# A two-layer RG-LRU and attention backbone with grouped experts: one written order past the end of the first experts, another order of the second layer's experts, and quarters of the output tiles for small blocks

## The chip, the cores and the metric

The kernel runs on one core of one Trainium2 chip. The metric is the device time of one execution in microseconds (us), lower is better. The names of the engines: PE multiplies matrices (TensorE), DVE is VectorE, ACT is ScalarE, POOL is GpSimd, SP is SyncE. SP only issues DMAs here; POOL issues the indirect DMAs (gathers and scatters) beside its own arithmetic.

## The reference, cut to what matters

Two layers over 256 latent tokens and 256 context tokens of 1024 numbers each, in float32. Layer 0 mixes with a recurrent block, layer 1 with grouped-query attention (the context is only read there). Behind each mixer stands a mixture of 16 experts, of which a router picks two for every token; the experts of layer 1 see the latent tokens alone.

```python
for i in range(DEPTH):                                     # DEPTH = 2
    hx = modulate(x, norm_mix_w[i], sh_m, sc_m)
    ...
    dx, dc = rglru_mixer(...) if i == 0 else attention_mixer(...)
    x = x + g_m * dx
    ...
    hx = modulate(x, norm_ffn_w[i], sh_f, sc_f)
    ...
    x = x + g_f * grouped_moe(hx, router_w, router_b, moe_w1[i], moe_w3[i], moe_w2[i])

def grouped_moe(h, router_w, router_b, w1, w3, w2):
    ...                                                    # gates: two of 16 experts per token, the others 0
    for e in range(N_EXPERTS):
        y = y + gates[..., e:e + 1] * ((jax.nn.silu(h @ w1[e]) * (h @ w3[e])) @ w2[e])
    return y
```

## The kernel before

**Layers and stages.** The program runs layer 0's mixer (to about 300 us), layer 0's experts (to about 608), layer 1's attention (`enter` and `Heads`, to about 790) and layer 1's experts (to the end). All weights are read once from HBM, in tiles of 2 MB, in two halves each, on SP's queue in one fixed order of jobs. A half is issued when its tile is free and when the fourth half before it has landed (`AHEAD = 4`).

**Experts.** The router's counts are known only at run time, so every expert place `e` has a fixed room. The first places (three in layer 0, four in layer 1) hold the experts 0 to 2 or 0 to 3. The others are filled by rank, the most wanted expert first: `ORDERS` says which rank stands at which place, `ROOM` how many rows a rank has room for, and `AGAIN` which ranks may have 128 rows more, in a branch (`tc.If`) that is skipped when it isn't needed. In layer 1 ranks 0 and 1 have room for 160 rows, worked as a block of 128 rows and a block of 32; every other rank has one block of 32 rows, and the four first places have one of 64. The places from 12 on are only worked if their expert has a token.

**One expert.** `fetch` clears a tile and gathers the expert's rows from HBM (POOL), `turn` transposes them (PE, with copies on ACT and DVE), `ups` multiplies by w1 and w3 (PE, line 945, tile `up`), ACT and DVE form the product `sx`, `flips` transposes it (PE) and copies it back (DVE, line 959), and `downs` multiplies by w2 (PE, line 977, tile `py`). DVE then multiplies with the gate into a tile `y` (line 985 in layer 1, line 988 in layer 0) and POOL adds these rows into HBM with an indirect DMA, the scatter (line 991). In the loop of `run`, place `e` does its `ups`, then the `downs` of place `e - 1`, then its own `flips`; places `e + 2` to `e + 5` are prepared in between.

**Scatters.** A scatter adds into the tensor that the scatter before it adds into, so each waits for the one before it to land. It reads `y`, so DVE may write that part of `y` again only when the scatter has landed. In layer 1 there are two such tiles, `ys[0]` and `ys[1]` (rows 2 and 3 of the tile `xr`, which is the name that the profile gives them), and `row` picks one of them.

**What sets the order.** Inside a `manual_schedule` region an engine runs its instructions in the order of the source; outside, a scheduler orders them by its own estimates. Each engine works its queue strictly in order. Through the experts the order of DVE, ACT, POOL and SP is manual, and PE's too.

**Between the layers.** After the last expert of layer 0, `leftover` holds work for rooms that were too small (skipped here). `enter` then splits the key and value weights (the third part of `qkv`) into a high and a low part, in eight pieces: `parts` copies a piece to `wkv` (ACT, line 1335) and subtracts for `wkvl` (DVE and POOL in turn, line 1336). SP loads the sums of layer 0 back from HBM (line 1364, `y<-yr`) once the last scatter has landed; DVE and POOL multiply them with a gain (line 1371), and the key and value products follow. The split of the query weights (`wq`, `wql`) is on ACT and POOL as well.

Of the kernel before, what the change touches and what calls it, by code (L numbers as in the profile page):

```python
# [15 lines left out]
ET = mybir.EngineType  # L16

D = 1024
NK = 8
# [15 lines left out]
ADA_AT = [32, 34]  # L35


ORDERS = [[11, 0, 10, 1, 9, 2, 8, 3, 7, 4, 6, 5, 12], [0, 2, 1, 3, 4, 5, 6, 7, 8, 9, 10, 11]]
ROOM = [[192, 128, 96, 96, 96, 96, 64, 64, 64, 64, 64, 64, 32], [160, 160, 32] + 9 * [32]]

AGAIN = [[1, 2, 3, 4, 6], [2, 3]]
# [21 lines left out]
BLOCKS = {0: (128, [(0, 0, 0)]), 1: (64, [(1, 0, 1)]), 2: (32, [(2, 0, 2)]), 3: (96, [(1, 0, 1), (2, 64, 3)])}  # L63
# [3 lines left out]
def base(i, k):  # L67

    return BASE if k < FIRST[i] else ROOM[i][ORDERS[i][k - FIRST[i]]]


def again(i, k):

    return k < FIRST[i] or ORDERS[i][k - FIRST[i]] in AGAIN[i]

# [12 lines left out]
def hybrid_kernel(ctx: ExitStack, tc: tile.TileContext, x, c, ctxt, c_ctx, ada_w, ada_b, norm_mix_w, norm_ffn_w,  # L88
# [3 lines left out]
    nc = tc.nc  # L92
# [5 lines left out]
    def open_banks(name):  # L98
        banks["ctx"] = ExitStack()
        banks["pool"] = banks["ctx"].enter_context(tc.tile_pool(reuse_waits="tile", name=name, bufs=8, space=PSUM))  # L100
# [72 lines left out]
    def done(key, more=True):  # L173
        pool = live.pop(key)[1]
        if more and (pool is not state.get("brief") or state["sent"] < LAST):
            send(pool)
        elif not more and state.get("later"):
            owed.append(pool)
# [390 lines left out]
    with tc.tile_pool(reuse_waits="tile", name="big0", bufs=1) as bp:  # L569
# [29 lines left out]
        with tc.tile_pool(reuse_waits="tile", name="n0", bufs=2) as n0, \  # L599
# [9 lines left out]
            parts = wp.tile([128, 4096], F32R, tag="w", name="parts")  # L609
# [101 lines left out]
        with tc.tile_pool(reuse_waits="tile", name="o0", bufs=2) as op:  # L711
            R0 = Router(0, [0, 1, 2, 3], op)
            pinned = tc.manual_schedule(engines={ET.PE})
# [7 lines left out]
    def moe(R, after=None):  # L721
        with ExitStack() as ctx2:
            if after is not None:
                state["brief"] = ctx2.enter_context(tc.tile_pool(reuse_waits="tile", name="weights0", bufs=1))
                send(state["brief"])
            moe_(R, ctx2.enter_context(tc.tile_pool(reuse_waits="tile", name=f"route{R.i}", bufs=1, side="right")),
                 after is not None)
        pinned.__exit__(None, None, None)
        if after is not None:

            for k in (("w1", E - 2), ("w3", E - 2), ("w2", E - 2), ("w1", E - 1)):
                done((k[0], R.i, k[1]), False)
            after(R.yr)

    def moe_(R, rp, early):
        i, chunks, conds, hr, yr, lg = R.i, R.chunks, R.conds, R.hr, R.yr, R.lg
# [4 lines left out]
        def places():  # L741

            xg = [rp.tile([128, D], F32, name=f"xg{a}") if i == 0 or a == 2 else xr[:, a, :] for a in range(NX)]
            xh = rp.tile([128, D], F32, name="xh")
            sx = [rp.tile([128, FF], F32, name=f"sx{a}") if i == 0 or a > 1 else None for a in range(4)]
            ys = [rp.tile([128, D], F32, name=f"y{a}") for a in range(3)] if i == 0 else [xr[:, 2 + a, :] for a in range(2)]
            for t in xg + sx[0:2] if i == 0 else []:
                nc.gpsimd.memset(t, 0.0)
            return xg, xh, sx, ys

        if i == 0:
            xg, xh, sx, ys = places()
# [86 lines left out]
        if i == 1:  # L839
            R.gf = rp.tile([128, D], F32, name="gf")  # L840
            xg, xh, sx, ys = places()
        ps1v = ps1.rearrange("p (c e) -> p c e", c=C)
        work = ExitStack()
# [116 lines left out]

        def row(e, b, bk):

            return ys[(e + b) % 2] if i or b == 0 else ys[2]

        def down(bk, aT, W2, ls, b, e):
# [136 lines left out]
            banks.pop("spare")  # L1102

        other = beside()
        work.enter_context(tc.manual_schedule(engines={ET.DVE, ET.Activation, ET.Pool, ET.SP}))
        warm = wk.tile([128, 1], F32, name="warm", bufs=1)
        busy(2)
        lists(0)
# [185 lines left out]
                    block(k, nk, room(i, k))  # L1294

        leftover()
        work.close()
        open_banks(f"psum{i + 1}")


    actx = ExitStack()

    def spare(name, dt=F32R):
        return wp.tile([128, 4096], dt, tag="w", name=name)

    def enter(yr):
# [13 lines left out]
        def wide(name, dt=F32R):  # L1320
            return spare(name, dt).rearrange("p (k f) -> p k f", k=NK)

        wkv, wkvl, hhi = wide("wkv"), wide("wkvl"), wide("hhi")
# [5 lines left out]
        ys = [misc[:, 1024 * z:1024 * z + 1024] for z in range(2)] + [yp.tile([128, D], F32, name=f"y{z}") for z in (2, 3)]  # L1329
        A, B = scale_vec(1, SC_M, 96, "am1"), vec(1, SH_M)  # L1330

        def parts(key, hi, lo, k, low):

            w = take(key).rearrange("p (k f) -> p k f", k=NK)[:, k, :]
            nc.scalar.activation(hi[:, k, :], w, AF.Copy)
            low.tensor_sub(lo[:, k, :], w, hi[:, k, :])

        with tc.manual_schedule(engines={ET.PE, ET.Activation, ET.DVE, ET.Pool}):
            for k in range(NK):
                parts(("qkv", 2), wkv, wkvl, k, (nc.vector, nc.gpsimd)[k % 2])  # L1340
            for j in (1, 0):
                spread(gf[j], vec(0, G_F), j)

# [303 lines left out]
    with ExitStack() as _:  # L1647
        with tc.tile_pool(reuse_waits="tile", name="o1", bufs=2) as op:
            R1 = Router(1, [2, 3], op)
            pinned = tc.manual_schedule(engines={ET.PE})  # L1650
# [8 lines left out]
def _constants():  # L1659
# [30 lines left out]
    for i in range(2):  # L1690
        k = FIRST[i]
        a[:, C_KEY + 16 * i:C_KEY + 16 * i + 16] = np.where(x < k, 65536 + 16384 * (k - 1 - x), E - 1 - x)
        a[:, C_RANK + 16 * i:C_RANK + 16 * i + 16] = list(range(k)) + [k + r for r in ORDERS[i]]
        a[:, C_ROOM + 16 * i:C_ROOM + 16 * i + 16] = [room(i, k) for k in range(E)]
# [32 lines left out]
```

## Time and profile before

| | |
|---|---|
| median of 3 runs | 1015.61 us (1012.28 to 1016.7) |
| the profiled execution, its own time | 1015.41 us |
| its span, first to last instruction | 1013.7 us |
| mean granted clock of PE, share of full | 0.927 |
| PE busy | 854.2 us, 84% |
| DVE busy | 488.6 us, 48% |
| ACT busy | 299.5 us, 30% |
| POOL busy | 252.4 us, 25% |
| HBM read and written | 290.85 MB and 14.81 MB, 302 GB/s over the span |

All times in the rows are from the span's start. The time beside the span, 1015.41 against 1013.7, is start and end that the trace does not show. An engine with a high busy share may still wait in single stages, so the shares say little about a change that acts in one stage; for that the waits and the timeline of the stage are read.

### The profile page before, as it was taken

The numbers are of one execution on the slowest core, as the hardware profiler recorded it, in microseconds if no ns is written. First come the engines' busy times: TensorE is split into PE (matmuls) and PEld (weight loads), VectorE is DVE, ScalarE is ACT, GpSimd is POOL, SyncE is SP. The second block draws the span as 40 slices with busy tenths as digits, with TensorE's granted clock in tenths as the row PEclk, the third lists the DMA queues.
The fourth block names the chain that finished last, engine by engine and source line by source line (L and its number), as shares of the span: only waits on it lengthen the run. The fifth ranks groups of instructions, "written<-read, shape, count | busy, mean of one in ns | idle before, by whom it ended". The sixth has DMA issues, their size and how long they took to land. (4 is left out here: it accounts for less than half of the span.)

```text
span 1013.7 us, 17132 instructions
## 1 busy us (share of the span) xinstructions
PE 854.2 (84%) x6495; PEld 538.8 (53%) x6495; DVE 488.6 (48%) x1366; ACT 299.5 (30%) x549; POOL 252.4 (25%) x193
## 2 busy tenths in 40 slices
PE   3789899889996999999998743879999689989953
PEld 2357675574454555456554413768654545545632
DVE  2878796652258632132221024587942664243452
ACT  3346556672012110011010012646851311110100
POOL 2272233300003320111211133652430223132232
PEclk9799999999997999999999967899999789999977
DMA  9956964899415899999999944221959589998970
GB/s 346 357 163 214 387 229 166 306 386 376 176 63 203 301 363 383 364 359 355 347 355 375 367 151 150 99 89 59 361 173 398 182 304 378 341 372 274 375 276 10
DMA packets 126926, 277.11 MB, mean 273 GB/s; under 512 B 7673, under 2 KB 12889, under 8 KB 126816
## 3 DMA queue, kind: packets, MB, share of 16 engines
q1 hardware_dynamic: 116064, 253.77, 68.4%
q0 software_dynamic: 8880, 15.54, 6.6%
q10 hardware_dynamic: 1872, 6.37, 1.6%
q8 instruction: 64, 1.05, 0.4%
q14 instruction: 46, 0.38, 0.1%
HBM read 290.85 MB, written 14.81 MB: 302 GB/s over the span
## 5 line engine op out<-in xcount | busy, mean ns | idle before, releaser
L945 PE MATMUL up<-w,xg 128*32 128x128 f32 (+2 forms) x1984 | 161.4, 338 | 10.1 <-DMA w<-in_moe_w_dram 9.4
L977 PE MATMUL py<-w,sx 128*32 128x256 f32 (+2 forms) x768 | 130.1, 521 | 19.1 <-DVE sx L959 17.9
L945 PEld LDWEIGHTS up<-w,xg 128*32 128x32 f32 (+2 forms) x1984 | 104.6, 127 | 60.4 <-issue 24.3
L950 DVE TENSOR_TENSOR sx<-sx,up 128x256 f32<-128x256 f32 (+3 forms) x31 | 13.4, 434 | 176.0 <-PE up L945 94.1
L977 PEld LDWEIGHTS py<-w,sx 128*32 128x32 f32 (+2 forms) x768 | 45.6, 135 | 84.9 <-issue 56.0
L949 ACT ACTIVATE sx<-up 128x256 f32<-128x256 f32 (+3 forms) x31 | 12.2, 395 | 230.5 <-PE up L945 217.5
L585 POOL TENSOR_TENSOR parts<-w,parts 128x1024 fp32r<-128x1024 f32 x16 | 40.3, 2520 | 113.0 <-DVE parts L584 105.0
L945 PE MATMUL up<-w,xr 128*32 128x128 f32 (+2 forms) x640 | 63.4, 351 | 0.6 <-ACT xr L508 0.6
L991 POOL DMA_INDIRECT yr<-y,yi x21 | 32.8, 1563 | 106.3 <-DVE y L988 37.1
L531 PE MATMUL bank<-w,yT 128*128 128x512 f32 x128 | 57.3, 595 | 0.0
L182 PE MATMUL bank<-hhi,parts 128*128 128x512 f32 x128 | 52.8, 412 | 4.2 <-DVE hhi L399 4.2
L183 PE MATMUL bank<-hlo,parts 128*128 128x512 f32 x128 | 52.1, 407 | 4.2 <-DVE hlo L400 2.2
L184 PE MATMUL bank<-hhi,parts 128*128 128x512 f32 x128 | 51.8, 405 | 1.3 <-POOL parts L585 1.3
L945 PEld LDWEIGHTS up<-w,xr 128*32 128x32 f32 (+2 forms) x640 | 38.5, 132 | 22.3 <-issue 15.6
L917 POOL DMA_INDIRECT xg<-hr,gi x21 | 20.8, 989 | 116.1 <-DVE f L908 67.9
L316 PE MATMUL bank<-w,st 128*32 128x512 f32 x384 | 46.4, 615 | 3.6 <-DMA w<-in_ada_w_dram 3.3
L932 ACT ACTIVATE xg<-tp 128x512 f32<-128x512 f32 x32 | 17.4, 594 | 84.8 <-PE tp L927 84.8
L465 DVE TENSOR_TENSOR rt<-bank,gm 128x512 f32<-128x512 f32 x12 | 8.3, 692 | 66.9 <-PE bank L531 66.9
L988 DVE TENSOR_SCALAR y<-py,gt 128x512 f32<-128x512 f32 (+1 forms) x21 | 14.4, 687 | 51.6 <-PE py L977 51.6
L985 DVE SCALAR_TENSOR_TENSOR xr<-py,gt,gf 32x256 f32<-32x256 f32 (+2 forms) x44 | 24.4, 554 | 30.6 <-PE py L977 19.7
L991 POOL DMA_INDIRECT out_dram<-xr,yi x14 | 22.1, 1581 | 64.4 <-DVE xr L985 19.6
L531 PEld LDWEIGHTS bank<-w,yT 128*128 128x128 f32 x128 | 23.4, 190 | 25.7 <-issue 25.5
(360 smaller groups left out, 1630.1 us busy)
## 6 DMA issues: line engine op xcount, KB each, us to landing
w<-in_moe_w_dram SPq DMA_DIRECT2D x192, 1024.0 KB
w<-in_ada_w_dram SPq DMA_DIRECT2D x48, 1024.0 KB
w<-in_lru_in_w_dram SPq DMA_DIRECT2D x8, 1024.0 KB
w<-in_attn_qkv_w_dram SPq DMA_DIRECT2D x6, 1024.0 KB
w<-in_lru_out_w_dram SPq DMA_DIRECT2D x4, 1024.0 KB
w<-in_attn_o_w_dram SPq DMA_DIRECT2D x4, 1024.0 KB
hr<-h ACTq DMA_DIRECT2D x6, 512.0 KB
yr<-zero POOLq DMA_DIRECT2D x4, 512.0 KB, 10.8
```

Source lines behind the costliest of these rows:

```text
L182: nc.tensor.matmul(pb, wh, xh, start=start, stop=False, skip_group_check=True)
L183: nc.tensor.matmul(pb, wh, xl, start=False, stop=False, skip_group_check=True)
L184: nc.tensor.matmul(pb, wl, xh, start=False, stop=stop, skip_group_check=True)
L316: nc.tensor.matmul(pa[32 * g:32 * g + 32, :], st[:, 4 * r + g, :], w[:, 4 * r + g, :], start=r == 0, stop=r == 1, skip_group_check=True, t ...
L531: nc.tensor.matmul(pb, src[:, k, n * 128:(n + 1) * 128], w[:, k, :], start=k == 0, stop=k == NK - 1)
L585: nc.gpsimd.tensor_sub(lo, w, h)
L917: nc.gpsimd.indirect_dma_start(out=dst[0:rows, :], out_offset=None, in_=hr[:, :], in_offset=bass.IndirectOffsetOnAxis(ap=idx[0:rows, :], a ...
L932: nc.scalar.activation(dst, pb, AF.Copy)
L945: nc.tensor.matmul(pw[g * Tn:(g + 1) * Tn, at:at + fg], hT[:, k, t0:t0 + Tn], W[:, k, g * fg:(g + 1) * fg], start=k == 0, stop=k == NK - 1 ...
L977: nc.tensor.matmul(py[j * Tn:(j + 1) * Tn, 0:wd], aT[:, ao + q * 128 + g * Tn:ao + q * 128 + (g + 1) * Tn], W2[:, f, j * dg + h * 512:j * ...
L985: nc.vector.scalar_tensor_tensor(dst[ps, :], py[ps, 0:wd], gate[ps, :], R.gf[ps, at:at + wd], ALU.mult, ALU.mult)
L991: nc.gpsimd.indirect_dma_start(out=yr[:, :].rearrange("r (g f) -> (r g) f", g=G), out_offset=bass.IndirectOffsetOnAxis(ap=ls.yi[:, z, b:b ...
```

## The change

Four edits. The order of DVE, ACT, POOL and SP in layer 0 stays manual beyond the experts, through `leftover` and the split of the key and value weights in `enter`, and so does PE's; the split thereby stands behind the experts' last instruction on each engine. In layer 1 the ranks stand in another order: the two ranks with 160 rows are at places 6 and 8 in place of 4 and 6, and the two with a branch at places 4 and 5 in place of 5 and 7. In layer 1 a block of 32 rows, which is 256 columns wide in `y`, goes into a quarter of `ys[e % 2]` that moves on with `e`, in place of the first 256 columns of `ys[(e + b) % 2]` (`b` is the block's number in its expert).

```diff
--- before.py
+++ after.py
@@ -35,7 +35,7 @@
 ADA_AT = [32, 34]
 
 
-ORDERS = [[11, 0, 10, 1, 9, 2, 8, 3, 7, 4, 6, 5, 12], [0, 2, 1, 3, 4, 5, 6, 7, 8, 9, 10, 11]]
+ORDERS = [[11, 0, 10, 1, 9, 2, 8, 3, 7, 4, 6, 5, 12], [2, 3, 0, 4, 1, 5, 6, 7, 8, 9, 10, 11]]
 ROOM = [[192, 128, 96, 96, 96, 96, 64, 64, 64, 64, 64, 64, 32], [160, 160, 32] + 9 * [32]]
 
 AGAIN = [[1, 2, 3, 4, 6], [2, 3]]
@@ -725,8 +725,9 @@
                 send(state["brief"])
             moe_(R, ctx2.enter_context(tc.tile_pool(reuse_waits="tile", name=f"route{R.i}", bufs=1, side="right")),
                  after is not None)
-        pinned.__exit__(None, None, None)
-        if after is not None:
+        if after is None:
+            pinned.__exit__(None, None, None)
+        else:
 
             for k in (("w1", E - 2), ("w3", E - 2), ("w2", E - 2), ("w1", E - 1)):
                 done((k[0], R.i, k[1]), False)
@@ -960,6 +961,9 @@
 
         def row(e, b, bk):
 
+            if i == 1 and BLOCKS[bk] == BLOCKS[2]:
+
+                return ys[e % 2][:, e // 2 % 4 * 256:]
             return ys[(e + b) % 2] if i or b == 0 else ys[2]
 
         def down(bk, aT, W2, ls, b, e):
@@ -1102,7 +1106,7 @@
             banks.pop("spare")
 
         other = beside()
-        work.enter_context(tc.manual_schedule(engines={ET.DVE, ET.Activation, ET.Pool, ET.SP}))
+        region.enter_context(tc.manual_schedule(engines={ET.DVE, ET.Activation, ET.Pool, ET.SP}))
         warm = wk.tile([128, 1], F32, name="warm", bufs=1)
         busy(2)
         lists(0)
@@ -1294,11 +1298,15 @@
                     block(k, nk, room(i, k))
 
         leftover()
+        if i == 1:
+            region.close()
         work.close()
         open_banks(f"psum{i + 1}")
 
 
     actx = ExitStack()
+
+    region = ExitStack()
 
     def spare(name, dt=F32R):
         return wp.tile([128, 4096], dt, tag="w", name=name)
@@ -1335,9 +1343,11 @@
             nc.scalar.activation(hi[:, k, :], w, AF.Copy)
             low.tensor_sub(lo[:, k, :], w, hi[:, k, :])
 
+        for k in range(NK):
+            parts(("qkv", 2), wkv, wkvl, k, (nc.vector, nc.gpsimd)[k % 2])
+        region.close()
+        pinned.__exit__(None, None, None)
         with tc.manual_schedule(engines={ET.PE, ET.Activation, ET.DVE, ET.Pool}):
-            for k in range(NK):
-                parts(("qkv", 2), wkv, wkvl, k, (nc.vector, nc.gpsimd)[k % 2])
             for j in (1, 0):
                 spread(gf[j], vec(0, G_F), j)
```

Three places in the order of instructions, as the two programs hold them (numbers of lines differ by 1 to 10 between the two, by what the diff adds).

DVE at the end of layer 0's experts, before: `wkvl` is the split, `sx<-pa` with 256 and 128 columns the `flips` of place 14, `y` the products for the scatters of places 14 and 15.

```order
L988 TENSOR_SCALAR y_2083<-py,gt 128x512
L1162 UNCONDITIONAL_BRANCH x2
L1336 TENSOR_TENSOR wkvl<-w,wkv 128x512 x2
L959 COPY sx_2077<-pa 128x256
L959 COPY sx_2077<-pa 128x128
L1336 TENSOR_TENSOR wkvl<-w,wkv 128x512 x2
L950 TENSOR_TENSOR sx_2078<-sx_2078,up 128x128
L988 TENSOR_SCALAR y_2081<-py,gt 128x512
L988 TENSOR_SCALAR y_2081<-py,gt 128x256
L959 COPY sx_2078<-pa 128x128
L988 TENSOR_SCALAR y_2082<-py,gt 128x256
```

The same place on DVE after the change:

```order
L992 TENSOR_SCALAR y_2083<-py,gt 128x512
L1166 UNCONDITIONAL_BRANCH x2
L960 COPY sx_2077<-pa 128x256
L960 COPY sx_2077<-pa 128x128
L951 TENSOR_TENSOR sx_2078<-sx_2078,up 128x128
L992 TENSOR_SCALAR y_2081<-py,gt 128x512
L992 TENSOR_SCALAR y_2081<-py,gt 128x256
L960 COPY sx_2078<-pa 128x128
L992 TENSOR_SCALAR y_2082<-py,gt 128x256
```

The two pairs of `wkvl` instructions are gone from between the experts' instructions; they come behind the branch of `leftover`.

POOL from the end of `leftover` on, before: `misc` is the gain, `hlo` the low part of the modulated tokens (the second `hlo` belongs to the second 128 latent tokens), `wql` the split of the query weights.

```order
L1371 TENSOR_TENSOR misc<-misc 128x1024 x2
L1405 TENSOR_TENSOR hlo_11878<-m,hhi 128x4x128
L1336 TENSOR_TENSOR wql<-w,wq 128x512 x6
L1405 TENSOR_TENSOR hlo_11878<-m,hhi 128x4x128
L1336 TENSOR_TENSOR wql<-w,wq 128x512 x6
L1405 TENSOR_TENSOR hlo_11878<-m,hhi 128x4x128
```

The same place on POOL after the change:

```order
L1344 TENSOR_TENSOR wkvl<-w,wkv 128x512 x4
L1381 TENSOR_TENSOR misc<-misc 128x1024 x2
L1415 TENSOR_TENSOR hlo_11876<-m,hhi 128x4x128
L1344 TENSOR_TENSOR wql<-w,wq 128x512 x8
L1415 TENSOR_TENSOR hlo_11876<-m,hhi 128x4x128
L1344 TENSOR_TENSOR wql<-w,wq 128x512 x3
L1415 TENSOR_TENSOR hlo_11876<-m,hhi 128x4x128
```

The four `wkvl` instructions stand here now, and the second `hlo` stands behind eight `wql` instructions in place of six.

DVE at the second expert with 160 rows in layer 1, with the semaphores that an instruction waits for in brackets (`DMASW` are those of POOL's DMAs), before: place 6, two halves of the block of 128 rows, then four pieces of the block of 32, then the `flips` of place 7.

```order
L985 SCALAR_TENSOR_TENSOR xr<-py,gt,gf 128x512 [waits DMASW6_49,DMASW1_49,PE_49]
L985 SCALAR_TENSOR_TENSOR xr<-py,gt,gf 128x512 [waits PE_49]
L985 SCALAR_TENSOR_TENSOR xr<-py,gt,gf 32x256 [waits DMASW5_49,PE_49]
L985 SCALAR_TENSOR_TENSOR xr<-py,gt,gf 32x256 x3
L959 COPY sx_13475<-pa 128x128 [waits PE_49]
L882 CAST r_15425<-ls 128x5 [waits PE_49]
L867 TENSOR_SCALAR oh<-io_b,psp 128x128 x2
L950 TENSOR_TENSOR sx_13473<-sx_13473,up 128x128 [waits PE_49,Activation_49]
```

The same after the change, at place 8:

```order
L989 SCALAR_TENSOR_TENSOR xr<-py,gt,gf 128x512 [waits PE_49]
L989 SCALAR_TENSOR_TENSOR xr<-py,gt,gf 128x512 [waits DMASW1_49,PE_49]
L989 SCALAR_TENSOR_TENSOR xr<-py,gt,gf 32x256 [waits DMASW5_49,DVE_49,PE_49]
L989 SCALAR_TENSOR_TENSOR xr<-py,gt,gf 32x256 x3
L960 COPY sx_13475<-pa 128x128 [waits PE_49]
L883 CAST r_15793<-ls 128x5 [waits PE_49]
L868 TENSOR_SCALAR oh<-io_b,psp 128x128 x2
L951 TENSOR_TENSOR sx_13473<-sx_13473,up 128x128 [waits PE_49,Activation_49]
```

The order within the expert is the same; the block of 32 rows (the third row) now lies in the same tile as the block of 128 and waits for a DMA and for DVE's own writes of the two rows above it.

## Rows read from the trace of the kernel before

**Rows 1.** Busy time in two windows: engine busy us (instructions), PEclk, DMA share, GB/s.

```profile
...
575.00:600.00 25.00, 6.28 (x80) 3.23 (x74) 5.49 (x7) 4.66 (x9) 5.26 (x4) 0.57 0.70 260
...
950.00:975.00 25.00, 16.14 (x355) 12.03 (x359) 11.79 (x49) 3.57 (x10) 7.73 (x7) 0.80 1.04 378
...
```

**Rows 2.** Timeline, 575 to 630: start, duration, instructions [idle before <- what ended it].

```profile
...
583.14 2.89 SPq L159 DMA_DIRECT2D w<-in_attn_qkv_w_dram  x2
593.50 2.19 ACT L1335 ACTIVATE wkv<-w 128x512 fp32r<-128x512 f32 x4 [25.99 <-DMA w<-in_attn_qkv_w_dram]
...
594.74 6.29 POOL L1336 TENSOR_TENSOR wkvl<-w,wkv 128x512 fp32r<-128x512 f32 x4 [21.23 <-ACT wkv L1335]
...
596.94 8.26 PE L977 MATMUL py<-w,sx 128*64 128x512 f32 x48 [14.45 <-DVE sx L959]
597.00 2.90 DVE L1336 TENSOR_TENSOR wkvl<-w,wkv 128x512 fp32r<-128x512 f32 x2
...
604.41 1.56 POOL L991 DMA_INDIRECT yr<-y,yi  x1 [3.39 <-DVE y L988]
...
609.88 1.55 POOL L991 DMA_INDIRECT yr<-y,yi  x1 [3.91 <-issue]
...
613.95 1.56 POOL L991 DMA_INDIRECT yr<-y,yi  x1 [2.52 <-DVE rope L1354]
...
619.52 0.82 SPq L1364 DMA_DIRECT2D y<-yr  x2
...
622.87 1.23 DVE L1371 TENSOR_TENSOR y<-y,misc 128x1024 f32<-128x1024 f32 x1 [9.07 <-DMA y<-yr]
...
626.84 5.09 POOL L1371 TENSOR_TENSOR misc<-misc 128x1024 f32<-128x1024 f32 x2 [11.33 <-DMA misc<-yr]
...
```

**Rows 3.** Timeline, 640 to 652.

```profile
...
646.70 2.19 POOL L1405 TENSOR_TENSOR hlo<-m,hhi 128x512 fp32r<-128x512 f32 x1 [0.36 <-DVE hhi L1404]
...
648.86 3.53 POOL L1336 TENSOR_TENSOR wql<-w,wq 128x512 fp32r<-128x512 f32 x2
...
648.94 0.50 PE L184 MATMUL bank<-wkv,hlo 128*128 128x512 f32 x1 [0.66 <-POOL hlo L1405]
...
```

**Rows 4.** Timeline of the later experts of layer 1, 908 to 975.

```profile
...
910.57 13.90 PE L945 MATMUL up<-w,xr 128*128 128x512 f32 x32
...
949.16 1.58 POOL L991 DMA_INDIRECT out_dram<-xr,yi  x1 [4.52 <-DVE xr L985]
...
950.17 3.70 PE L945 MATMUL up<-w,xg 128*32 128x128 f32 x128
...
957.26 4.00 PE L945 MATMUL up<-w,xr 128*32 128x128 f32 x128
...
960.08 1.56 POOL L991 DMA_INDIRECT out_dram<-xr,yi  x1 [9.34 <-PE up L945]
...
968.42 1.97 DVE L985 SCALAR_TENSOR_TENSOR xr<-py,gt,gf 32x256 f32<-32x256 f32 x4 [10.51 <-DMA out_dram<-xr,yi]
...
970.66 1.58 POOL L991 DMA_INDIRECT out_dram<-xr,yi  x1 [6.82 <-DVEq L1162]
...
970.95 0.22 PE L897 MATMUL pa<-r,dup_b 128*128 128x5 bf16 x3 [8.67 <-DVE r L882]
...
```

**Rows 5.** Timeline of the last experts of layer 1, 940 to 1004.

```profile
...
974.93 3.70 PE L945 MATMUL up<-w,xr 128*32 128x128 f32 x128
...
980.34 1.57 POOL L991 DMA_INDIRECT out_dram<-xr,yi  x1 [5.40 <-PE tp L927]
...
980.57 0.22 PE L897 MATMUL pa<-r,dup_b 128*128 128x5 bf16 x3
...
1001.45 1.59 POOL L991 DMA_INDIRECT out_dram<-xr,yi  x1 [4.60 <-DVEq L1229]
```

**Rows 6.** The chain that ended last, one piece near its end.

```profile
...
992.23 3.56 DMA out_dram<-xr,yi
...
```

**Rows 7.** Busy time in five-microsecond windows near the end.

```profile
...
980.00:985.00 5.00, 3.01 (x45) 1.88 (x43) 3.98 (x18) 1.51 (x4) 3.52 (x3) 0.98 0.38 106
...
```

## The prediction

> **What bounds the kernel now.** I read the busy shares first, then the windows, then the timeline where the change acts. PE is busy 84% of the span, so only stretches in which PE idles can give much. Two such stretches touch the change.
>
> The first is the end of layer 0's experts. From 575 to 600 PE works 6.28 of 25 us at a granted clock of 0.57 [rows 1]. The timeline says why: the second product of place 14 begins at 596.94 after 14.45 us idle, released by DVE's copy of `sx` [rows 2]. That copy stands behind two pieces of the `wkvl` split on DVE (first order), and these wait for ACT's copies, which start at 593.50, after 25.99 us of waiting for the load of the key and value weights [rows 2]. So a late load of layer 1 holds back the last experts of layer 0. Behind them the chain is serial: scatters at 604.41, 609.88 and 613.95, each after the landing of the one before, then SP's load of the sums at 619.52, then the gains on DVE (622.87) and POOL (626.84) [rows 2]. Nothing of layer 1 can start without them, so what the first product gains, the rest inherits.
>
> Then the query split's neighbour: the first product with the second `hlo` at 648.94 came 0.66 us after PE was free, released by POOL [rows 3]. POOL is just in time there.
>
> The second stretch is the tail of layer 1's experts. From 950 to 975 PE works 16.14 us of 25 [rows 1]. PE idles 8.67 us before 970.95, because DVE is held 10.51 us, until 968.42, by the landing of the scatter issued at 960.08 [rows 4]: place 7's `y` reuses the part that this scatter reads. The last scatter goes out at 1001.45 [rows 5].
>
> **The change, part by part.**
>
> *The split behind the experts.* The product at 596.94 then waits for its own weights and `sx` alone. SP's issue at 583.14 waited for the fourth half before it, the first half of place 14's w2, and the second issue, at 583.14 + 2.89 = 586.03 at the latest, for the second half [rows 2]. So the product can start between 583.14 and 586.03, 13.8 to 10.9 us sooner. I take 12.5, since part of the block runs before the second half is needed. But the first scatter then goes out at 604.41 − 12.5 = 591.9, while the key and value weights still stream. A scatter there landed in 5.47 us (604.41 to 609.88) with an idle stream [rows 2], and one under the stream, later in the program, took 8.3 (960.08 to 968.42) [rows 4]. I take 7, nearer the middle, since the stream ends soon after; 1.5 us go back. Sum −11.0. Bounds: −13.8 with nothing given back; −5.5 if only 10.9 is gained and two of the three landings (the last took 5.57, 613.95 to 619.52 [rows 2]) rise to 8.3, 2.7 more each.
>
> *The split itself* costs nothing where it now stands. ACT's copies wait for the load as before. DVE's four pieces (2.90 for two [rows 2]) take 5.8 us between its last `y`, about 602 (the last scatter, 613.95, less 11 and a little), and its gain, about 622.87 − 11 = 611.9. POOL's four take 6.29 [rows 2] from about 604.5, behind the last scatter at 603, until 610.8; its gain is wanted at 626.84 − 11 = 615.8. The cover is the landing of the last scatter and the load behind it. Were it gone, up to 3 us of the pieces would show.
>
> *The second `hlo`* now stands behind eight `wql` pieces in place of six (second order). Two cost 3.53 us on POOL [rows 3], and POOL had no slack there. PE may do other products first, so the bounds are 0 and 3.5; I take +2.7.
>
> *Layer 1's order and quarters.* Quarters give place 7 a part of `y` that no scatter in flight reads, so its 10.51 us are gone. But the block of 32 rows of a 160-row expert now lies in the tile of its own block of 128 and waits for that scatter to land (third order: the row with `DMASW5_49` now follows DVE's own writes of the same tile). Queued behind that `y` on DVE are the next place's `flips` copy, the list cast `r` and the next `sx`; PE's next `downs` waits for the first two, POOL's next scatter for `y`. At place 6 this lies beside place 8's 128-row `ups` of 13.90 us [rows 4], so nothing shows; without that cover it would cost up to the 8.67 that such a wait cost before. At place 8 the next `ups` takes 3.70 us, so it shows.
>
> Its time: the second 160-row expert's first scatter was at 949.16 [rows 4]. Two small experts now come ahead of it. Each takes between 7.09 (`ups` at 950.17 and 957.26 [rows 4]) and 9.68 (scatters at 970.66 [rows 4] and 980.34 [rows 5]); I take the middle, 8.4, since these two lie between large blocks. So 949.16 + 16.8 = 966.0. Landing: 10.92 (949.16 to 960.08, a block of this size under the stream [rows 4]), so 976.9. The rest is as it was after place 7's wait: 2.53 us until PE goes on (968.42 to 970.95 [rows 4]) and, from `downs(9)`, 20.88 (980.57 to 1001.45 [rows 5]). 976.9 + 23.4 = 1000.3 against 1001.45: −1.2. So a wait of about this size only moves from place 7 to place 8. Bounds: +1.4 with two cycles of 9.68. Below, a landing of 3.56, as the last one took [rows 6]: then no wait shows at all, and −8.7, the 8.67 of PE, are gained.
>
> The Trainium skill, "DMA: Bandwidth & Descriptors", section "Anatomy of one DMA", prices a DMA at about 2.0 us plus its bytes at 436 GB/s. For 512 KB my estimate from that page is 3.2 us; by it the sum would end at the −8.7. The trace agrees late in the tail, when the DMA engines' share is 0.38 (3.56 us [rows 6, 7]), and not at a share of 1.04 [rows 1], where 8.3 to 10.9 us were taken [rows 4]. The same page ("Issuing engines are not separate DMA queues") has all DMAs interleave on the same 16 engines, as those rows suggest.
>
> **Sum.** −11.0 + 0 + 2.7 − 1.2 = −9.5 on the profiled 1015.41, which is 0.2 under the median: 1005.9 us.
>
> **The rivals.**
>
> *R1, the wait at place 8 is short.* If the stream is over or thin when place 8's scatter goes out, it lands in 3.56 and lies beside `ups(10)`. For: the stream thins by 980 [rows 7]. Against: at 966 it was full [rows 1]. Time: −11.0 + 2.7 − 8.7 = −17.0, 998.4 us.
>
> *R2, the gain at the entry is mostly lost.* All scatters land under the stream and POOL's `hlo` costs its full 3.5: −5.5 + 3.5 − 1.2 = −3.2, 1012.2 us, no change that can be told. For: the key and value load runs until about 593.50 [rows 2]. Against: that is only 1.6 us after the first scatter goes out.
>
> *R3, slower: the two small experts placed early run at the scatters' pace.* POOL's queue is strict, so a scatter that waits for the one before it holds the gathers behind it, and thereby the next `ups`. If places 4 and 5 so cost 17.67 us each (957.26 to 974.93, the cycle with the wait [rows 4, 5]), place 8's scatter goes out at 984.5, the end is at 984.5 + 10.92 + 23.4 = 1018.8, +17.4 in place of −1.2: 1015.41 − 8.3 + 17.4 = 1024.5 us. It decides from cycles of 15.8 us on (two of them and the same rest give +13.6, which brings the sum to 0.5% over before). Against: landings of 8 to 11 us do not fill such a cycle.
>
> **How the numbers follow.** About 0.5%, 5 us, is what a measurement of this kernel can tell from no change. Chances: the forecast 0.60 (own range 1002 to 1010: entry between −13.8 and −8, tail within its bounds, `hlo` 0 to 3.5), R1 0.18, R2 0.17, R3 0.05. The range of 8 in 10 takes in R1 to 996 and R2 to 1012.5, and leaves out R3 and the ends. Faster: forecast and R1, 0.78. Same: R2, 0.17. Slower: 0.05.
>
> **What would show it.** Right: PE's 14.45 us before place 14's second product gone or under 4; SP's load of the sums near 608; DVE's wait before place 7's `y` gone; a DVE wait of about 10 us before the 32-row `y` of places 6 and 8, with PE idle at place 8 alone, for 6 to 9 us; PE waiting some 3 us for POOL's second `hlo` near 638. Wrong: place 14's product still late for another reason (a list, a gather); scatters at the entry landing in 8 us or more; POOL's `wkvl` releasing the first key product; PE waiting for weights at places 4 to 6, where small experts now use them up faster.

## The result and the profile after

The changed kernel took 997.6 us in the median of four runs (996.72 to 1000.39), the kernel before 1015.0 in runs beside it: the ratio is 0.9836, with a 95% interval of 0.9806 to 0.9866. Taken again beside other kernels it was 1000.34 against 1014.01, ratio 0.9854 (0.983 to 0.9877). So the change is worth 14 to 17 us by the medians, where 9.5 were forecast. The measured time lies under the forecast's own range of 1002 to 1010 us and inside the wide one, which goes down to 996.

| | before | after |
|---|---|---|
| profiled execution, own time | 1015.41 us | 1000.39 us |
| span | 1013.7 us | 998.7 us |
| mean granted clock of PE | 0.927 | 0.933 |
| PE busy | 854.2 us, 84% | 854.6 us, 86% |
| DVE, ACT, POOL busy | 488.6, 299.5, 252.4 us | 488.5, 300.3, 253.8 us |

No engine's work has changed by more than 1.4 us; what went is idle time. To see where, I cut the two spans at events that both have: layer 0's fifth-last scatter, SP's load of the sums, the first expert's 64-row `ups` of layer 1, and the last scatter. Each column is the time from the event before, in us.

| kernel | to the fifth-last scatter | to SP's load | to the first expert | to the last scatter | to the end | span |
|---|---|---|---|---|---|---|
| before | 562.78 | 56.74 | 188.61 | 193.32 | 12.25 | 1013.7 |
| after | 563.28 | 45.22 | 188.57 | 190.43 | 11.20 | 998.7 |
| after, again | 563.39 | 44.90 | 188.59 | 191.25 | 11.27 | 999.4 |

The entry of layer 1 gave 11.52 us, the tail of layer 1 2.89, the attention between them nothing, and the ends about half a microsecond: 15.0 in all.

The entry first, on the timeline of the changed kernel from 570 to 630 (columns as in [rows 2], to which these answer).

```profile
...
580.90 1.94 PE L946 MATMUL up<-w,xg 128*32 128x128 f32 x32 [2.71 <-DMA w<-in_moe_w_dram]
...
583.57 1.97 PE L981 MATMUL py<-w,sx 128*64 128x512 f32 x4 [0.73 <-DMA w<-in_moe_w_dram]
...
586.29 6.17 PE L981 MATMUL py<-w,sx 128*64 128x512 f32 x44 [0.75 <-DMA w<-in_moe_w_dram]
...
591.67 1.55 POOL L995 DMA_INDIRECT yr<-y,yi  x1 [17.61 <-DVE y L992]
...
594.07 2.19 ACT L1343 ACTIVATE wkv<-w 128x512 fp32r<-128x512 f32 x4 [18.23 <-DMA w<-in_attn_qkv_w_dram]
...
598.55 1.55 POOL L995 DMA_INDIRECT yr<-y,yi  x1 [5.33 <-issue]
...
602.45 2.14 POOL L995 DMA_INDIRECT yr<-y,yi  x1 [2.34 <-DVE rope L1364]
...
608.50 0.82 SPq L1374 DMA_DIRECT2D y<-yr  x2
608.54 5.90 POOL L1344 TENSOR_TENSOR wkvl<-w,wkv 128x512 fp32r<-128x512 f32 x4 [3.96 <-DMA yr<-y,yi]
...
611.82 1.49 DVE L1381 TENSOR_TENSOR y<-y,misc 128x1024 f32<-128x1024 f32 x1 [5.25 <-DMA y<-yr]
...
615.45 6.17 POOL L1381 TENSOR_TENSOR misc<-misc 128x1024 f32<-128x1024 f32 x2 [1.01 <-DMA misc<-yr]
...
```

PE's second product of place 14 starts at 583.57, not 596.94, and the 14.45 us of idle time before it are gone. It runs as its weights land: four matmuls with the first half, 0.75 us of waiting, the rest with the second. The scatters go out at 591.67, 598.55 and 602.45, so the first landed in 6.88 us, counted, as in the prediction, to the issue of the next. ACT copies `wkv` when its load has landed, as before. POOL's `wkvl` pieces begin at 608.54, when the last scatter has landed, and its gain follows at 615.45, after 1.01 us of waiting for its data: the cover was just enough.

The attention next, on the list of what PE waited for, by line (total us, times, longest), of the changed kernel.

```profile
...
PE bank L184 <- POOL hlo L1415: 4.0, 1, 4.0
...
PE bank L1507 <- DVE misc L1501: 0.7, 1, 0.7
...
```

PE now waits 4.0 us for POOL's `hlo`. The list of the kernel before shows 0.7 there, and another wait, which has shrunk:

```profile
...
PE bank L1497 <- DVE misc L1491: 4.2, 2, 2.8
...
PE bank L184 <- POOL hlo L1405: 0.7, 1, 0.7
...
```

Line 1497 there is line 1507 after the change: PE's wait for the query heads went from 4.2 to 0.7 us. The two changes nearly cancel; experiment 8 asks whether one wait takes the other's place.

The tail, at place 6 and then at place 8 (timeline; these answer to [rows 4, 5]).

```profile
...
916.84 1.59 POOL L995 DMA_INDIRECT out_dram<-xr,yi  x1 [4.69 <-DVE xr L989]
...
918.69 13.90 PE L946 MATMUL up<-w,xg 128*128 128x512 f32 x32
...
926.56 1.97 DVE L989 SCALAR_TENSOR_TENSOR xr<-py,gt,gf 32x256 f32<-32x256 f32 x4 [10.01 <-DMA out_dram<-xr,yi]
...
```

```profile
...
940.12 1.96 DVE L989 SCALAR_TENSOR_TENSOR xr<-py,gt,gf 32x256 f32<-32x256 f32 x4
...
953.28 1.57 POOL L995 DMA_INDIRECT out_dram<-xr,yi  x1 [4.54 <-DVE xr L989]
...
954.30 3.82 PE L946 MATMUL up<-w,xr 128*32 128x128 f32 x128
...
962.56 1.96 DVE L989 SCALAR_TENSOR_TENSOR xr<-py,gt,gf 32x256 f32<-32x256 f32 x4 [9.55 <-DMA out_dram<-xr,yi]
...
964.80 1.55 POOL L995 DMA_INDIRECT out_dram<-xr,yi  x1 [9.94 <-DVE xr L989]
...
964.97 0.22 PE L898 MATMUL pa<-r,dup_b 128*128 128x5 bf16 x3 [5.82 <-DVE r L883]
...
965.12 3.45 PE L981 MATMUL py<-w,sx 128*32 128x256 f32 x32
...
971.19 3.24 PE L981 MATMUL py<-w,sx 128*32 128x256 f32 x32 [2.33 <-DVE sx L960]
...
987.50 1.59 POOL L995 DMA_INDIRECT out_dram<-xr,yi  x1 [6.07 <-DVEq L1233]
```

At place 6 DVE is held 10.01 us until 926.56, 9.72 us after the scatter went out, and PE is in the 128-row `ups` from 918.69 to 932.59: hidden. Place 7's `y` starts at 940.12 with no idle time in its row, where it waited 10.51 us before. At place 8 the scatter of the 128 rows goes out at 953.28, the `y` of the 32-row block starts when it has landed, 9.28 us later, at 962.56 after 9.55 us of DVE's idle time, and PE resumes at 964.97 after 5.82 us. The windows of the changed kernel (columns as in [rows 1]) show the stream of weight loads full at place 6, with a DMA share of 1.02 and 1.06. At place 8 it ends during the wait, the DMA share falling from 1.03 to 0.29, and PE's granted clock is 0.64 and 0.68 around and after its idle time.

```profile
...
915.00:920.00 5.00, 5.00 (x49) 2.65 (x48) 0.75 (x1) 1.50 (x4) 1.59 (x1) 1.00 1.02 391
920.00:925.00 5.00, 5.00 (x13) 2.26 (x12) 0.00 (x0) 0.01 (x1) 0.00 (x0) 1.00 1.06 299
...
955.00:960.00 5.00, 4.14 (x120) 3.75 (x110) 0.00 (x0) 1.48 (x5) 0.00 (x0) 1.00 1.03 327
960.00:965.00 5.00, 0.03 (x2) 0.03 (x2) 2.34 (x7) 0.30 (x1) 0.20 (x1) 0.64 0.29 80
965.00:970.00 5.00, 3.86 (x38) 1.74 (x37) 4.80 (x21) 0.00 (x0) 3.29 (x3) 0.68 0.15 17
...
```

The products `downs(9)` and `downs(10)` (with w2, of places 9 and 10) take 3.45 and 3.24 us there; the windows' clock lies between the two levels (1.2 and 2.4 GHz), nearer to the lower.

### The profile page after: what moved, and what is told of

It reads as the page before. It is cut to its first block, busy times and chain, and to the rows that moved or that the text cites. A ratio compares the mean times of both kernels' runs of the same rounds, so it can differ in the third digit from the quotient of the medians.

```text
span 998.7 us, 17124 instructions
## 1 busy us (share of the span) xinstructions
PE 854.6 (86%) x6495; PEld 541.9 (54%) x6495; DVE 488.5 (49%) x1366; ACT 300.3 (30%) x549; POOL 253.8 (25%) x193
## 5 line engine op out<-in xcount | busy, mean ns | idle before, releaser
L946 PE MATMUL up<-w,xg 128*64 128x256 f32 (+2 forms) x1888 | 171.7, 345 | 9.9 <-DMA w<-in_moe_w_dram 8.9
L946 PEld LDWEIGHTS up<-w,xg 128*64 128x64 f32 (+2 forms) x1888 | 107.2, 128 | 67.3 <-issue 31.8
L946 PE MATMUL up<-w,xr 128*32 128x128 f32 (+2 forms) x736 | 51.2, 315 | 1.4 <-issue 0.9
L946 PEld LDWEIGHTS up<-w,xr 128*32 128x32 f32 (+2 forms) x736 | 35.5, 120 | 14.5 <-issue 9.5
L933 ACT ACTIVATE xg<-tp 128x512 f32<-128x512 f32 x32 | 17.4, 594 | 84.7 <-PE tp L928 72.2
L531 PEld LDWEIGHTS bank<-w,yT 128*128 128x128 f32 x128 | 23.4, 190 | 25.7 <-issue 25.5
L1610 POOL TENSOR_SCALAR pe<-pe,mx 128x512 f32<-128x512 f32 x16 | 25.0, 1566 | 45.0 <-DVE mx L1605 29.7
```

What stands on the lines that cost most here:

```text
L531: nc.tensor.matmul(pb, src[:, k, n * 128:(n + 1) * 128], w[:, k, :], start=k == 0, stop=k == NK - 1)
L946: nc.tensor.matmul(pw[g * Tn:(g + 1) * Tn, at:at + fg], hT[:, k, t0:t0 + Tn], W[:, k, g * fg:(g + 1) * fg], start=k == 0, stop=k == NK - 1 ...
L1610: (nc.gpsimd if u else nc.vector).tensor_scalar(pe, pe, mx[:, 1:2], None, ALU.mult)
```

## The experiments

Ratios are to the kernel before on the same chip, its median 1013.42 for the first four, 1014.01 for the next four and 1013.67 for the last three. The stage table of the changed kernel goes on here with each one's profiled run.

| kernel | to the fifth-last scatter | to SP's load | to the first expert | to the last scatter | to the end | span |
|---|---|---|---|---|---|---|
| long order alone | 560.99 | 45.39 | 188.06 | 192.05 | 11.81 | 998.3 |
| ranks alone | 563.82 | 57.59 | 188.32 | 187.02 | 11.25 | 1008.0 |
| quarters alone | 562.93 | 55.11 | 189.19 | 191.20 | 11.57 | 1010.0 |
| ranks and quarters | 560.53 | 56.93 | 189.30 | 187.55 | 11.99 | 1006.3 |
| after without quarters | 560.82 | 45.67 | 187.42 | 187.85 | 11.54 | 993.3 |
| after, other tile | 561.80 | 45.64 | 187.94 | 185.21 | 11.31 | 991.9 |
| other tile, old ranks | 560.10 | 46.97 | 188.48 | 183.59 | 11.46 | 990.6 |
| after, hlo on DVE | 563.87 | 46.23 | 187.80 | 189.79 | 11.31 | 999.0 |
| before, split on POOL | 562.21 | 56.48 | 188.76 | 190.31 | 11.84 | 1009.6 |

The first column, which no edit touches, varies by 3.8 us from run to run. The tail of the three kernels with the ranks and tiles of before (before, long order alone, split on POOL) varies between 190.31 and 193.32. So a difference of less than 3 us in a single profile's tail cannot be told from none, and the 2.89 above is of that size; below, the timed ratios decide.

**1. The longer order alone.** The changed kernel with two edits undone:

```diff
-ORDERS = [..., [2, 3, 0, 4, 1, 5, 6, 7, 8, 9, 10, 11]]
+ORDERS = [..., [0, 2, 1, 3, 4, 5, 6, 7, 8, 9, 10, 11]]
...
-            if i == 1 and BLOCKS[bk] == BLOCKS[2]:
-                return ys[e % 2][:, e // 2 % 4 * 256:]
```

> Only the longer written order; ranks and output tiles as before. Theory (three separate terms): SP's load of the sums leaves near 608.5, 11 us sooner than the 619.5 of before, POOL's second hlo holds PE some 4 us and the query heads give about 3.5 back, so layer 1's first expert starts 11 us sooner and the time is 11 us under before, about 1004 us; the wait of 10.5 us before place 7's y is still there. Rival (the entry's gain is partly a gain of the tail, because an earlier entry meets another stream): more than 13 us or less than 8 us.

999.79 us, ratio 0.9877 (0.9847 to 0.9907), which is 9 to 16 us. The theory's 11 lies in that, but the medians are 13.6 apart, beyond the rival's 13, so the times alone do not part the two. The stages speak for the theory: SP's load left 45.39 us after the fifth-last scatter against 56.74, 11.35 sooner, the tail is that of before, and DVE still waits 10.09 us before place 7's `y`. So the entry's term stands by itself.

**2. The ranks alone, 3. the quarters alone, 4. both,** on the kernel before.

```diff
# 2 and 4
-ORDERS = [..., [0, 2, 1, 3, 4, 5, 6, 7, 8, 9, 10, 11]]
+ORDERS = [..., [2, 3, 0, 4, 1, 5, 6, 7, 8, 9, 10, 11]]
# 3 and 4
+            if i == 1 and BLOCKS[bk] == BLOCKS[2]:
+                return ys[e % 2][:, e // 2 % 4 * 256:]
```

> Only layer 1's ranks in the new order, without quarters and without the longer order. Theory: the wait of place 7 moves to place 9, whose y reuses the part that place 8's second scatter reads; it ends 8.3 us after a scatter at about 975, and three scatters follow in 17.5 us: -0.4 us, and to -5 if that scatter already lands in 4 us. So 1010 to 1015 us. Rival (the order alone is what helps in the tail, as less work follows the wait): -8 us or more, 1007 us.

> Only the quarters, with the ranks and the order of before. Theory: place 7's wait of 10.5 us goes, but the 32-row y of place 6 now waits about 10 us for its own 128-row scatter beside an ups of 3.70 us, so PE idles some 6 us at its place; -1 us, within 3 of before. Rival (the new wait is cheap, and the old one is simply gone): -8.7 us, about 1006 us.

> Ranks and quarters together, without the longer order. Theory: the tail is worth what the changed kernel shows, -2.9 us from layer 1's first expert to the last scatter, so about 1012 us, with PE idle some 6 us at place 8 and none at place 6. Rival (the part of the gain over the 14 us of the two terms comes from here): -6 us, about 1009 us.

Ranks alone: 1007.18 us, ratio 0.9948 (0.9923 to 0.9973), 3 to 8 us faster. The time is under the 1010 to 1015 that the theory gave, and the interval takes in its best case of 5 and ends just short of the rival's 8. The wait moved to place 9 as the theory said. Quarters alone: 1013.06, ratio 1.0 (0.9977 to 1.0022), nothing, as the theory had it. Both: 1007.63, ratio 0.9948 (0.993 to 0.9966), 3 to 7 us: what the ranks alone give. Here the theory missed: it took the 2.9 us from the changed kernel's profile, and the rival's 6 is nearer. PE idles 5.67 us at place 8, as expected.

With the quarters alone, DVE's timeline and PE's show the new wait at place 6, where the next `ups` is short:

```profile
...
955.66 1.97 DVE L988 SCALAR_TENSOR_TENSOR xr<-py,gt,gf 32x256 f32<-32x256 f32 x4 [10.64 <-DMA out_dram<-xr,yi]
...
```

```profile
...
958.07 0.22 PE L897 MATMUL pa<-r,dup_b 128*128 128x5 bf16 x3 [7.04 <-DVE r L882]
...
```

DVE is held 10.64 us and PE 7.04, in place of the 10.51 and 8.67 of before [rows 4]: the wait has moved one place. With the ranks alone it moves to place 9, and there it costs less (POOL, DVE, PE):

```profile
...
964.11 1.57 POOL L991 DMA_INDIRECT out_dram<-xr,yi  x1 [4.54 <-DVE xr L985]
...
975.03 1.56 POOL L991 DMA_INDIRECT out_dram<-xr,yi  x1 [9.35 <-issue]
...
978.88 1.97 DVE L985 SCALAR_TENSOR_TENSOR xr<-py,gt,gf 32x256 f32<-32x256 f32 x4 [4.89 <-DMA out_dram<-xr,yi]
...
981.22 3.64 PE L977 MATMUL py<-w,sx 128*32 128x256 f32 x32 [7.90 <-DVE sx L959]
...
```

DVE is held 4.89 us. This scatter of 32 rows landed in 3.85 us (975.03 to 978.88), with the stream nearly over (DMA share 0.19 from 975 to 980); one of the same size took 8.34 under the full stream before (960.08 to 968.42 [rows 4]). PE is idle 7.90 us before `downs(10)`, but 2.92 of it stand there in experiment 6 too, where no `y` waits for a scatter. So the wait costs PE some 5.0 us, against 8.67 before.

The rows also say what two small experts are worth on either side. From layer 1's first expert to the first scatter of the second 160-row expert it is 154.38 us here (964.11 − 809.73, the sum of the first three columns), and was 141.03 before (949.16 − 808.13, [rows 4]): the two ahead cost 6.7 us each. From that scatter to the last it is 32.64 us (to 996.75), and was 52.29 (to 1001.45, [rows 5]), which is 9.8 less for each of the two. That is not the cost of an expert, because the shorter wait, some 3.7 us, is in it; without it, 8.0 each is left. So some 3.7 of the 6.3 us by which this profile's tail is shorter come from the wait, and where the rest comes from is not shown. The tail's gain is that of the ranks, and the quarters add none to it.

**5. The changed kernel again, 6. with the other tile, 7. without quarters, 8. with `hlo` on DVE,** side by side.

```diff
# 6: the block of 32 rows of a 160-row expert goes into a quarter of the tile that its 128 rows do not use
-                return ys[e % 2][:, e // 2 % 4 * 256:]
+                return ys[(e + b) % 2][:, (e // 2 + 2 * b) % 4 * 256:]
# 7
-            if i == 1 and BLOCKS[bk] == BLOCKS[2]:
-                return ys[e % 2][:, e // 2 % 4 * 256:]
# 8
-                (nc.vector, nc.gpsimd)[h].tensor_sub(hlo[:, ks, ts], m, hhi[:, ks, ts])
+                nc.vector.tensor_sub(hlo[:, ks, ts], m, hhi[:, ks, ts])
```

> The changed kernel once more, to have it beside the next three on one chip. Theory: -11 us of the entry and -6 us of ranks and quarters, about 17 us under before; the first profile's tail (-2.9 us) was a slow one, and this one's lies between -3 and -6.

> The changed kernel, but the 32-row block of a 160-row expert goes into a quarter of the other tile, so that its y waits for no scatter in flight. Theory (the wait at place 8 is a price of the change): PE's 5.8 us before downs(9) go, and the lower clock behind that idle time with them: 6 to 9 us faster than the changed kernel. Rival (POOL's queue: the second scatter waits for the first to land anyway, and the gathers behind it): under 2 us.

> The changed kernel without the quarters: longer order and new ranks, y in the parts of before. Theory (quarters only move the wait): place 9's y now waits for place 8's second scatter, which lands in 4 to 6 us since the weight stream is over; within 3 us of the changed kernel. Rival (the quarters carry the tail's gain): 6 us slower.

> The changed kernel with the low part of the modulated tokens (hlo) on DVE alone, so that none stands behind wql on POOL. Theory (my +2.7 was a real term that another one covered): PE's wait of 4.0 us for hlo goes and 3 to 4 us are gained. Rival (it is no term, since the products behind it wait for something else): under 1 us, or DVE's added work shows.

The changed kernel: 1000.34 us, ratio 0.9854 (0.983 to 0.9877), which is 12 to 17 us; the 17 that were expected stand at the end of that. Its profile's tail is 2.1 us under that of before, not 3 to 6.

The other tile: 992.17 us, ratio 0.9789 (0.9769 to 0.9809), 8.2 us under the changed kernel by the medians and 6.6 by the ratios, both in the 6 to 9 of the theory. Its timeline at place 8 (compare 953.28 to 965.12 above):

```profile
...
951.58 1.57 POOL L995 DMA_INDIRECT out_dram<-xr,yi  x1 [4.54 <-DVE xr L989]
...
952.94 1.97 DVE L989 SCALAR_TENSOR_TENSOR xr<-py,gt,gf 32x256 f32<-32x256 f32 x4 [1.65 <-PE ls L879]
...
958.44 0.22 PE L898 MATMUL pa<-r,dup_b 128*128 128x5 bf16 x3
...
958.59 1.93 PE L981 MATMUL py<-w,sx 128*32 128x256 f32 x32
...
961.52 1.56 POOL L995 DMA_INDIRECT out_dram<-xr,yi  x1 [8.37 <-DVE gt L913]
...
963.88 3.47 PE L981 MATMUL py<-w,sx 128*32 128x256 f32 x32 [2.92 <-DVE sx L960]
...
980.59 1.59 POOL L995 DMA_INDIRECT out_dram<-xr,yi  x1 [6.21 <-DVEq L1233]
```

The `y` of the 32 rows starts at 952.94, 1.36 us after the scatter of the 128 rows, not 9.28; PE goes from `ups` to `downs(9)` with no idle time in its row, and that product takes 1.93 us where it took 3.45. The second scatter still stands on POOL until 961.52, as the rival said, but the profile shows nobody waiting for it. With experiment 10 this is the fastest version here.

Without quarters: 997.77 us, ratio 0.985 (0.9828 to 0.9872), which overlaps the changed kernel's: within 3 us of it, as the theory had it. The wait sits at place 9, takes 4.43 us on DVE and leaves PE idle for 7.45, 4.5 more than the 2.92 of experiment 6:

```profile
...
963.01 1.97 DVE L986 SCALAR_TENSOR_TENSOR xr<-py,gt,gf 32x256 f32<-32x256 f32 x4 [4.43 <-DMA out_dram<-xr,yi]
...
```

`hlo` on DVE: 997.17 us, ratio 0.9849 (0.9826 to 0.9872). That is 3.2 us under the changed kernel by the medians and 0.5 by the ratios, so the times alone do not decide between 3 to 4 us and nothing. The stage does, as far as one profile tells: from SP's load to the first expert it took 187.80 us, against 188.57 and 188.59. PE's 4.0 us for `hlo` are gone from its list, and the wait for the query heads is back at the size that it had before the change:

```profile
...
PE bank L1507 <- DVE misc L1501: 4.2, 2, 2.8
...
```

So the 3 to 4 us were not gained in that stage, and the theory of this run fell. The two waits are alternatives: the term was not 2.7 us but under 1.

**9. The split on POOL alone,** on the kernel before.

```diff
-                parts(("qkv", 2), wkv, wkvl, k, (nc.vector, nc.gpsimd)[k % 2])
+                parts(("qkv", 2), wkv, wkvl, k, nc.gpsimd)
```

> The kernel before with all eight wkvl pieces on POOL, none on DVE; order, ranks and tiles as before. They stand on POOL ahead of place 14's scatter. Theory (two gates stood in a row: DVE's pieces ahead of the flips, POOL's ahead of the scatter): PE's second product of place 14 starts near 584, 13 us sooner, but the scatter waits for eight pieces from 594.7 on, 12.6 us, so it leaves near 607, 3 us later than before: 0 to +3 us. Rival (DVE's two pieces are the whole cause): the scatter leaves near 592, -11 us.

1012.73 us, ratio 1.0 (0.9979 to 1.0022), as the theory had it. Its timeline:

```profile
...
583.01 1.97 PE L977 MATMUL py<-w,sx 128*64 128x512 f32 x4 [0.73 <-DMA w<-in_moe_w_dram]
...
585.47 4.46 PE L977 MATMUL py<-w,sx 128*64 128x512 f32 x12 [0.49 <-DMA w<-in_moe_w_dram]
...
594.01 9.86 POOL L1336 TENSOR_TENSOR wkvl<-w,wkv 128x512 fp32r<-128x512 f32 x8 [20.70 <-ACT wkv L1335]
595.88 2.19 ACT L1335 ACTIVATE wkv<-w 128x512 fp32r<-128x512 f32 x4 [0.39 <-DMA w<-in_attn_qkv_w_dram]
...
598.16 3.64 PE L977 MATMUL py<-w,sx 128*32 128x256 f32 x32 [8.23 <-ACTq L1162]
...
604.03 1.56 POOL L991 DMA_INDIRECT yr<-y,yi  x1 [0.16 <-issue]
...
618.69 0.82 SPq L1364 DMA_DIRECT2D y<-yr  x2
...
```

With DVE's pieces away, the product starts at 583.01, as in the changed kernel, but the first scatter goes out at 604.03 (604.41 before), behind POOL's eight pieces, which end at 603.87. And the 32-row product of the same place waits 8.23 us for ACT, whose copies of `wkv` end at 598.07. So three queues held work of the next stage ahead of the chain: DVE's, POOL's and ACT's. Moving DVE's share to POOL gave nothing; the change clears all three. This run does not clear DVE alone, since it doubles the pieces that POOL holds. With POOL's own four pieces, which ended at 601.03 before (594.74 + 6.29 [rows 2]), the scatter could have left some 3 us sooner (an estimate from those rows; not run), not 12.7.

**10. The other tile with the ranks of before.** Experiment 6 with the old list of ranks.

```diff
-ORDERS = [..., [2, 3, 0, 4, 1, 5, 6, 7, 8, 9, 10, 11]]
+ORDERS = [..., [0, 2, 1, 3, 4, 5, 6, 7, 8, 9, 10, 11]]
```

> As p5_other_tile (no y waits for a scatter in flight), but with the ranks of before. Theory (the ranks pay because small experts behind the wait cost some 9.8 us each and ahead of it some 7): without the wait the order is worth little, within 2 us of p5_other_tile. Rival (the order pays by itself, through loads or gathers): 4 us or more slower than p5_other_tile.

993.42 us, ratio 0.9809 (0.9774 to 0.9843): over experiment 6 by 1.3 us in the medians and 2.0 in the ratios, each to the kernel before on its own chip. The intervals overlap, so without a wait the order of the ranks is worth nothing that can be told, though the interval does not shut out the rival's 4 us. That fits with ranks that pay by a shorter wait.

**11. Two loads in flight.** The changed kernel with `AHEAD = 2`.

> The changed kernel with two weight halves in flight in place of four. It measures the landing of the scatters under the stream, on which both terms rest. Theory (a scatter's packets queue behind what the loads have queued): with half as much in flight the scatter of place 8's 128 rows lands in 5 to 7 us, in place of 9 to 11, and the kernel may lose elsewhere by thinner loads. Rival (the share of bandwidth decides, not what is queued): still 9 to 11 us while the DMA share is about 1.

1027.77 us in one run. At place 8, on the timeline and in three windows:

```profile
...
972.66 1.58 POOL L995 DMA_INDIRECT out_dram<-xr,yi  x1 [4.54 <-DVE xr L989]
...
983.68 1.97 DVE L989 SCALAR_TENSOR_TENSOR xr<-py,gt,gf 32x256 f32<-32x256 f32 x4 [11.29 <-DMA out_dram<-xr,yi]
...
```

```profile
...
970.00:975.00 5.00, 5.00 (x87) 2.89 (x89) 0.75 (x1) 0.00 (x0) 1.58 (x1) 1.00 1.01 340
975.00:980.00 5.00, 3.40 (x96) 3.03 (x89) 0.00 (x0) 1.78 (x5) 0.00 (x0) 1.00 1.02 258
980.00:985.00 5.00, 0.00 (x0) 0.00 (x0) 1.29 (x3) 0.00 (x0) 0.00 (x0) 0.85 0.86 278
...
```

The scatter of 972.66 had landed at 983.68, in 11.02 us, while the DMA share was 1.01, 1.02 and 0.86. The theory of queued loads fell: with half as much in flight the landing was not shorter, 11.02 us against 9.28 at place 8 and 9.72 at place 6 of the changed kernel. The whole was some 27 us slower than the changed kernel, in this one run.

## Why the prediction was right, and which terms were off

**The entry, −11.0: right, step by step.** The product came 13.4 us sooner (12.5 taken, 13.8 the bound), the first scatter at 591.67 (591.9), its landing took 6.88 us (7), SP's load left 11.0 us sooner. Experiment 1 gives it alone. What the prediction did not say is that DVE's pieces were one gate of three (experiment 9); it named them alone for PE's delay, and a change that only moved them to POOL was worth nothing.

**The split at no cost: right.** POOL's pieces ended at 614.44, four microseconds later than I placed them, since POOL waited for the last scatter to land, which I had not counted; its gain still came with its data.

**The second `hlo`, +2.7: this term failed.** The wait came at nearly the size that I gave it, 4.0 us in place of 0.7, but the stage from SP's load to the first expert took 188.57 us against 188.61. PE lost 3.3 us there and gained 3.5 at the query heads. I had priced a wait without asking which later wait it would replace, so the term came to nothing in the stage. Experiment 8 shows the exchange the other way round. Which common cause stands behind both is not settled; ACT and POOL both work on the query split there.

**The tail, −1.2: right in mechanism, mis-sized.** The wait did move from place 7 to place 8, hidden at 6 and exposed at 8, with 5.82 us of PE against 8.67. On the clock of before, that is with the 11.06 us added by which layer 1's first expert came sooner (797.07 against 808.13, the sums of the first three columns), place 8's scatter went out at 953.28 + 11.06 = 964.34, so the two small experts cost 7.6 us each, not 8.4: −1.7. The landing took 9.28, not 10.92: −1.6. The stream ended during it, but the scatter of the same size at place 6 took 9.72 under a full stream, so the end of the stream as the reason is not shown. From there to the end it was 24.94 us, not 23.4: +1.5, as much as `downs(9)` lost at the lower clock (3.45 against 1.93 in experiment 6). Together −1.2 − 1.7 − 1.6 + 1.5 = −3.0, against −2.89 in this profile. By the timed runs the tail gives more, 3 to 7 us (experiment 4). I had costed ranks and quarters as one; the ranks make the gain, alone or with the quarters, and experiment 2 puts some 3.7 of the 6.3 us in its profile down to a shorter wait of PE. On top of the long order the two cannot be told from nothing: the changed kernel's ratios of 0.9836 and 0.9854 lie within the interval of the long order alone (0.9847 to 0.9907) or overlap it with their own.

**Sum.** −9.5 forecast; without the `hlo` term and with the tail as measured, −11.5 − 2.9 and half a microsecond of ends, −15.0. The rest to the median's −17.4 is not explained by any stage; the second taking of the same kernel gave −13.7, so it lies within the spread of runs. By the timed parts the sum is much the same: 9 to 16 us for the entry alone (experiment 1) and 3 to 7 for ranks and quarters (experiment 4).

**Where the number fell, and luck.** 997.6 is 0.8 us from R1's 998.4 and outside the forecast's own range, which was drawn too narrow: its bound of the entry with no `hlo` term, −13.8 − 1.2 = −15.0, already gives 1000.4. The wide range held the time only because it was drawn to take in R1, and R1's mechanism did not happen. So the steps at the entry were foreseen; that the time fell inside the wide range at this end was luck, made of a lost `hlo` term, a larger tail and the spread of runs.

**The rivals.** R1 (a short wait at place 8) did not happen: the stream did end, with a DMA share of 0.29 in the window in which the scatter landed, and it still took 9.28 us. Its price was read from the wrong scatter. The 3.56 us of [rows 6] belong to the last but one scatter, of 32 rows, a quarter of the bytes of 128 rows, and the DMA share where it landed was 0.10 (992 to 996), not the 0.38 of [rows 7]. So the trace did not agree there with an estimate for 512 KB, and no run shows a scatter of 128 rows without a stream. R1's rule, the price of about 2.0 us plus bytes from the Trainium skill, "DMA: Bandwidth & Descriptors", section "Anatomy of one DMA", does not hold under a full stream in any run here. For 128 rows the traces have 10.92 us before, 9.72 at place 6 of the changed kernel and 11.02 in experiment 11. What R1 would have been worth is near experiment 6: 6.6 to 8.2 us, against the 7.5 between it and my forecast. R2 fell with the entry. R3's cycles of 17.67 us did not come; 7.6 was measured.

## What to carry to other kernels

When instructions of the next stage wait for a late load inside this stage's queues, look through every queue that the chain passes, not the first one that the timeline names: here DVE, POOL and ACT each held it, and moving DVE's share to POOL gave nothing. Before a new wait is added to the sum, find the wait of the same engine behind it, because a delay that another wait covers is no term. A buffer cut finer to lift one wait needs a look at who else writes it: sending the second block of an expert to the other tile was worth some 7 to 8 us on top of the change, while without a wait the order of the experts was worth nothing that could be told.

## What the hardware showed that I had not expected

A scatter of 32 rows landed in 3.85 us at a DMA share of 0.19 (experiment 2) and in 8.34 under a full stream (before). For 128 rows, halving the weight loads in flight left the landing at 11.02 us under a DMA share of 1.02 to 0.86; with four loads in flight it took 9.72 under a share of 1.02 to 1.06, and 9.28 where the stream ended during it. Around and behind 5.82 us without work PE was granted a clock of 0.64 and 0.68 in two windows of five microseconds, and a product of 32 rows took 3.45 us in place of the 1.93 that it took where PE came to it without a pause.
